# A transformer block on one core: every engine in source order from the expert queries on, with dependent steps spaced by units

## The chip, the cores and the metric

The kernel runs on one core of one Trainium2 chip. A core has TensorE (PE, matmuls), VectorE (DVE), ScalarE (ACT), GpSimd (POOL) and SyncE (SP, which here only issues DMAs), each with its own queue of instructions. The metric is the device time of one execution in microseconds; less is better.

## The reference

One layer on 256 tokens of width 2048, in float32: a mixer (sliding-window attention and an mLSTM, gated and merged), and then an expert retrieval (PEER) on the normed result. The change lies in the second part, which is this:

```python
xn = rms_norm(x)                                     # x: (256, 2048)
qp = (xn @ w_peer_q).reshape(T, 8, 2, 128)           # 8 heads, two halves
scores = einsum('thcd,hcnd->thcn', qp, peer_keys)    # 128 keys per half
s_top, i_top = top_k(scores, 16)
cand = s_top[:, :, 0, :, None] + s_top[:, :, 1, None, :]
top_s, pos = top_k(cand.reshape(T, 8, 256), 16)      # expert = i0 * 128 + i1
gates = softmax(top_s)
act = gelu(einsum('td,thkd->thk', xn, peer_u[idx]))  # exact gelu
out = x + einsum('thk,thkd->td', gates * act, peer_v[idx])
```

There are 16384 experts, so `peer_u` and `peer_v` have 16384 rows of 2048 numbers each.

## The kernel before

The retrieval is computed densely for 224 of the 256 tokens (ND). All of `u` is streamed once: 128 blocks of 128 experts ("expert i" below is such a block), each as two **units** of 128x1024 weights. A unit is loaded by SP into `raw` (4 buffers), split into two fp32r parts, `hi` by ScalarE (L89) and `lo` by VectorE (L90, from raw and hi), with 2 buffers each, and multiplied by TensorE: eight matmuls of hi with both parts of the tokens (L818) and eight of lo (L823). After an expert's second unit `sum_u` adds the two halves of the PSUM tile into `z` (ScalarE copy L214, VectorE add L215), and `act_u` takes the Gelu (L795, L797) into `W` (`wA` for the experts 0 to 79, `wB` for the others). The gates of each token are scattered into `W` four tokens at a time by `scatter`: VectorE compares a one-hot `A` (L1020), ScalarE makes a one-hot `B` times the gate with two activations per token (L1024, L1025), four matmuls multiply them (L1029), and VectorE (L1040) or ScalarE (L1042) puts the product into `W`. Where Gelu values already stand, it multiplies; where they don't yet, it copies and `act_u` multiplies later (L798). Then all of `v` is streamed in 256 units (L1090, L1092), with `W` split into a `ring` of fp32r entries (`split_w`).

The first 32 tokens (SP = 32) are computed by gathering: POOL fetches their experts' rows (`fetch`, L919) into six `slab` buffers, VectorE makes a dot product for each u row (`dot`, L949) and adds each weighted v row (`add_row`, L975). There are 128 such rows in each direction.

Ahead of the u stage come the queries: 32 units of `w_pq` (L174, L178), `score` (L767, L768) and the ranking, all of it on VectorE: `top16`, `pick16`, `decode`, `gates`, `lookup`, `turn`.

Stages are lists of units. `run` loads and splits the next unit and then calls `step` for the one before it. `step` first issues the unit's matmuls, then what was put in the list `later` in the step before, then one row of `rows_todo` when `pace[1]` reaches 1 (it grows by `row_rate` per unit), and then entries of `side`, as many as `pace[0]` pays for: it grows by the stage's rate per unit, is capped at 4, and each entry has a cost. `E0` is the expert from which the gates are scattered: the first run ends there, `drain` empties both lists, the ranking's memory is given back, and the second run begins.

The order of instructions on an engine is set by a planner, which puts ready instructions first by its own estimate of times. Before the change only VectorE is taken from it, from the queries to the end:

```python
    dve_order = tc.manual_schedule(engines={mybir.EngineType.DVE})
    dve_order.__enter__()
```

Under it VectorE runs its instructions in the order in which the source issues them. The queues of ScalarE, TensorE, POOL and SP are ordered by the planner (the gathers alone are kept in order by `keep`).

Of the kernel before, what the change touches and what calls it, by code (L numbers as in the profile page):

```python
# [8 lines left out]
F32 = mybir.dt.float32  # L9
# [3 lines left out]
AF = mybir.ActivationFunctionType  # L13
# [27 lines left out]
def hybrid_block_kernel(ctx: ExitStack, tc: tile.TileContext, a, out):  # L41
# [82 lines left out]
    def drain():  # L124
        flush()
        while side:
            tick()
# [18 lines left out]
    def run(units, rate=1.0):  # L146

        ready = None  # L150
        for u in units:
            nxt = (parts_of(load(u[0])), u[1])
            if ready:
                step(*ready, rate)
            ready = nxt
        if ready:
            step(*ready, rate)
# [571 lines left out]
        V.memset(part[c * SP:(c + 1) * SP], float(c))  # L729
    pair = exc.tile([P, SP], F32, name="pair")  # L730
    V.tensor_reduce(pair, ident.rearrange("p (c t) -> p t c", c=PARTS), axis=AX.X, op=OP.add)
    NSL = 6
    slab = [exc.tile([P, HD], F32, name=f"slab{j}") for j in range(NSL)]
    NA = 80
    wA = exc.tile([P, NA, ND], F32, name="wA")
# [2 lines left out]
    def load_xg():  # L738
        nc.sync.dma_start(wA[:, 0:KT], xgd)

    def norm_xg(c):
        xs = wA[:, 4 * c:4 * c + 4]
        V.tensor_mul(xs, xs, rb[:, SP:].unsqueeze(1).to_broadcast([P, 4, ND]))

    side += [(0.1, load_xg)] + [(1.0, lambda c=c: norm_xg(c)) for c in range(KT // 4)]
    second = []

    tks = ExitStack()
# [8 lines left out]
    def top16(vals, ov, oi):  # L757
        V.max(out=ov[:, 0:8], in_=vals)
        V.max_index(oi[:, 0:8], ov[:, 0:8], vals)
        V.match_replace(vals, ov[:, 0:8], vals, LOW)  # L760
        V.max(out=ov[:, 8:16], in_=vals)
        V.max_index(oi[:, 8:16], ov[:, 8:16], vals)

    def score(n, q):
        p2 = psd.tile([P, QU], F32, name="sd")
        for t in range(NT):
            PE.matmul(p2[:, t * NK:(t + 1) * NK], q[:, t * P:(t + 1) * P], keysT[:, n], start=True, stop=True)  # L767
        S.activation(sc[:, :, n], p2[:, 0:NT * NK].rearrange("p (t k) -> p t k", k=NK), AF.Copy)  # L768
        for t in range(NT):
            (side, second)[t].append((1.7, lambda t=t: top16(sc[:, t, n], st_[:, t, n], it_[:, t, n])))  # L770

    def evac_q(n):
        def g(ps):
            q = eb.tile([P, T], F32, name="z")
            total(q, ps[:, :T], ps[:, T:])
            V.tensor_mul(q, q, rb)
            later.append(lambda: score(n, q))
        return lambda ps: later.append(lambda: g(ps))
# [3 lines left out]
    def wv(i):  # L782
        return W[0][:, i] if i < NA else W[1][:, i - NA]
# [1 line left out]
    done = {"tok": 0, "e": 0}  # L785

    def sum_u(i, ps):
        z = eb.tile([P, ND], F32, name="z")
        total(z, ps[:, :ND], ps[:, ND:2 * ND])
        later.append(lambda: act_u(i, z))  # L790

    def act_u(i, z):
        k = done["tok"]
        if k < ND:
            S.activation(wv(i)[:, k:], z[:, k:], AF.Gelu)  # L795
        if k > 0:
            S.activation(z[:, :k], z[:, :k], AF.Gelu)  # L797
            V.tensor_mul(wv(i)[:, :k], wv(i)[:, :k], z[:, :k])  # L798
        done["e"] = i + 1

    own = {}
# [24 lines left out]
            return f  # L826
        return [(a["u"][i][:, h * HU:(h + 1) * HU], consume(i, h)) for i in range(i0, i1) for h in range(KT // per)]

    E0 = 66


    a16 = tk.tile([P, TOPK], F32, name="a16")
# [55 lines left out]
        V.tensor_mul(gv, gv, gs[:, 1].unsqueeze(2).to_broadcast([P, PH, TOPK]))  # L888

    def turn(t):  # L890
        pi = psd.tile([P, QU], F32, name="sd")
        for c in range(3):
            PE.transpose(pi[:, c * P:(c + 1) * P], iv[:, c], ident)
        V.tensor_copy(i0T[:, t * P:(t + 1) * P], pi[:, 0:P])
        V.tensor_scalar(i1T[:, t * P:(t + 1) * P], pi[:, P:2 * P], -1.0, None, op0=OP.mult)
        V.tensor_copy(gT[:, t * P:(t + 1) * P], pi[:, 2 * P:3 * P])
        V.tensor_scalar(ngT[:, t * P:(t + 1) * P], pi[:, 2 * P:3 * P], -1.0, None, op0=OP.mult)

    keep = tc.keep_in_program_order
    tables = {"u": a["ur"], "v": a["v"].rearrange("e (c d) -> (e c) d", d=HD)}

    def turn_to_grid():
# [11 lines left out]

    def fetch(table, s):
        ix = own["ix"]
        keep(G.indirect_dma_start(out=slab[s % NSL], out_offset=None, in_=tables[table],  # L919
                                  in_offset=bass.IndirectOffsetOnAxis(ap=ix[:, s:s + 1], axis=0)))  # L920

    def quarter_rows(dst, src):

# [55 lines left out]
    def choose():  # L979
        own["oh"] = tk.tile([P, 2, HG, TOPK, TOPK], F32, name="oh", tag="keysT")  # L980
        for t in range(NT):
            if t:
                side.extend(second)
            side.extend([(1.9, lambda t=t, h=h: pick16(t, h)) for h in range(PH)])
            side.extend([(2.6, lambda t=t: decode(t)), (0.9, lambda t=t: gates(t))])
            side.extend([(1.2, lookup(t, c, g)) for c in range(2) for g in range(2)])
            side.append((1.3, lambda t=t: turn(t)))
            if t == 0:
                side.extend([(1.0, own_index)] + [(1.0, lambda: None)] * 3 + [(0.5, own_rows)])
        own_x()  # L990

    def first(f, u):

        def g(parts):
            f()
            u[1](parts)
        return (u[0], g)

    row_rate[0] = 0.5
    dve_order = tc.manual_schedule(engines={mybir.EngineType.DVE})  # L1000
    dve_order.__enter__()
    units = []
    for n in range(2 * PH):
        units += ws_units(a["w_pq"][n], X2, evac_q(n))
    ue = u_units(0, E0)
    ue[0] = first(turn_to_grid, ue[0])
    ue[2] = first(choose, ue[2])
    run(units + ue, 1.0)
    drain()
    tks.close()  # L1010

# [4 lines left out]
    def scatter(t0):  # L1016

        A = eb.tile([P, TG, NK], F32, name="A")
        B = eb.tile([P, TG, NK], F32, name="B")
        V.tensor_tensor(A, iot.unsqueeze(1).to_broadcast([P, TG, NK]),  # L1020
                        i0T[:, t0:t0 + TG].unsqueeze(2).to_broadcast([P, TG, NK]), op=OP.is_equal)
        for j in range(TG):
            t = t0 + j
            S.activation(B[:, j], iot, AF.Square, bias=i1T[:, t:t + 1])  # L1024
            S.activation(B[:, j], B[:, j], AF.Relu, bias=gT[:, t:t + 1], scale=ngT[:, t:t + 1])  # L1025
        yield
        ps = psd.tile([P, TG, NK], F32, name="sd")
        for j in range(TG):
            PE.matmul(ps[:, j], B[:, j], A[:, j], start=True, stop=True)  # L1029
        yield  # L1030
        m = done["e"]
        c0 = t0 - SP
        for s, (lo, hi) in enumerate(((0, NA), (NA, NE))):
            for x0, x1, mul in ((lo, min(max(m, lo), hi), True), (max(min(m, hi), lo), hi, False)):
                if x1 <= x0:
                    continue
                dst = W[s][:, x0 - lo:x1 - lo, c0:c0 + TG]
                src = ps[:, :, x0:x1].rearrange("p t i -> p i t")
                if mul:
                    V.tensor_mul(dst, src, dst)  # L1040
                else:
                    S.activation(dst, src, AF.Copy)  # L1042
        done["tok"] = c0 + TG

    side += [(0.7, scatter(t0)) for t0 in range(SP, T, TG)]
    left = 2 * (NE - E0) - 6
    row_rate[0] = len(rows_todo) / left
    run(u_units(E0, NE), (ROW * len(rows_todo) + 2.1 * len(side)) / left)
    drain()
    while rows_todo:  # L1050
        rows_todo.pop(0)()

# [26 lines left out]
    def v_consume(i, h):  # L1081
        def f(parts):
            if i == 0:
                acc[h] = [(psd, pmm)[j % 2].tile([P, QU], F32, name=("sd", "mm")[j % 2]) for j in range(NB2)]
            if i % EG == 1:
                split_w((i - 1 + EG) % NE)
            hi, lo = parts
            both = ring[:, i % NR].rearrange("p s t -> p (s t)")
            for j in range(NB2):
                PE.matmul(acc[h][j][:, :2 * ND], hi[:, j * P:(j + 1) * P], both, start=(i == 0), stop=False)  # L1090
            for j in range(NB2):
                PE.matmul(acc[h][j][:, :ND], lo[:, j * P:(j + 1) * P], ring[:, i % NR, 0],  # L1092
                          start=False, stop=(i == NE - 1))
            if i == NE - 1:
                for j in range(NB2):
                    total(outT[h][j], acc[h][j][:, :ND], acc[h][j][:, ND:2 * ND])
        return f
# [16 lines left out]
            nc.sync.dma_start(out[0:SP, c * HD:(c + 1) * HD], own["x"][c * SP:(c + 1) * SP])  # L1114

    units = [(a["v"][i * P:(i + 1) * P, h * HU:(h + 1) * HU], v_consume(i, h)) for h in range(2) for i in range(NE)]
    ow = own_weights()
    next(ow), next(ow), next(ow, None)
    split_w(0)
    rows_todo += [lambda s=s: add_row(s) for s in range(NS)]  # L1120
    row_rate[0] = NS / (len(units) - 12)
    pace[1] = 0.0
    units[NE + 40] = first(load_x1, units[NE + 40])
    units[-3] = first(own_out, units[-3])
    run(units)
    flush()
    assert not rows_todo
    for q in range(4):
        finish(q)
    dve_order.__exit__(None, None, None)  # L1130


# [61 lines left out]
```

## Time and profile before

| | |
|---|---|
| time, median of 3 runs | 2233.15 us (2232.91 to 2233.73) |
| time of the profiled execution | 2231.89 us, its span 2230.1 us |
| TensorE matmul, weight load busy | 2132.3 us (96%), 1938.7 us (87%) |
| VectorE, ScalarE, GpSimd busy | 1689.4 (76%), 1283.9 (58%), 389.7 us (17%) |
| mean granted TensorE clock | 0.988 of full speed |
| DMA | 487.22 MB, mean 218 GB/s |

The time lies 1.8 us over the span, which counts from the first to the last instruction. TensorE's busy time comes from modelled ends of pipelined matmuls; the granted clock tells how far it ran at full speed. Stages by their first matmul: queries at 679.9, u at 799.0, the first scatter matmul at 1165.1, v at 1571.1 us.

### The profile page before, as it was taken

What the parts mean: (1) busy time and instruction counts of PE and PEld (TensorE: products, weight loads), DVE (VectorE), ACT (ScalarE), POOL (GpSimd) and SP (SyncE); (2) the same over time, 40 slices, a digit from 0 to 9 for tenths busy, and PEclk for the clock granted to TensorE, in tenths of its full rate; (3) what the DMA queues carried; (4) which work ended last, traced back from release to release, by engine and by line L of the source; (5) the groups of instructions that cost most, each with busy time, mean ns of one, the idle gap of its engine ahead of it and who ended that gap; (6) DMA issues with size and microseconds to landing.
All of it is one profiled execution on the core that took longest, in us unless ns stands there. A gap on an engine that the chain in (4) does not pass through costs nothing. (4 is left out here: it accounts for less than half of the span.)

```text
span 2230.1 us, 35017 instructions
## 1 busy us (share of the span) xinstructions
PE 2132.3 (96%) x12836; PEld 1938.7 (87%) x12836; DVE 1689.4 (76%) x2905; ACT 1283.9 (58%) x2238; POOL 389.7 (17%) x324
## 2 busy tenths in 40 slices
PE   6999999999997988999998999999999999999998
PEld 5887778888886878899888988889899999999998
DVE  7987687878886778788886777777677777777776
ACT  5755566556543444555558887887445555555544
POOL 3000000000031002333332222220322222322210
PEclk9999999999998999999999999999999999999999
DMA  5565544555575545777675665665777877877774
GB/s 201 189 190 169 166 159 163 179 190 186 199 249 197 171 153 177 255 262 257 234 244 197 216 218 203 217 217 203 250 262 266 262 269 262 292 263 267 262 260 162
DMA packets 138892, 487.22 MB, mean 218 GB/s; under 512 B 17712, under 2 KB 19968, under 8 KB 138240
## 3 DMA queue, kind: packets, MB, share of 16 engines
q1 hardware_dynamic: 115520, 415.43, 54.8%
q0 software_dynamic: 20896, 67.73, 9.5%
q8 instruction: 100, 1.64, 0.3%
q10 hardware_dynamic: 2304, 1.84, 0.2%
q14 instruction: 72, 0.59, 0.1%
HBM read 478.88 MB, written 6.05 MB: 217 GB/s over the span
## 5 line engine op out<-in xcount | busy, mean ns | idle before, releaser
L90 DVE TENSOR_TENSOR lo<-raw,hi 128x1024 fp32r<-128x1024 f32 x762 | 943.3, 1239 | 422.1 <-ACT hi L89 410.8
L89 ACT ACTIVATE hi<-raw 128x1024 fp32r<-128x1024 f32 x762 | 802.6, 1057 | 642.2 <-PE mm L1090 316.5
L818 PE MATMUL mm<-X,hi 128*128 128x448 f32 x2048 | 473.2, 374 | 26.5 <-ACT hi L89 21.4
L818 PEld LDWEIGHTS mm<-X,hi 128*128 128x128 f32 x2048 | 370.8, 191 | 57.7 <-ACT hi L89 28.3
L1090 PE MATMUL sd<-X,hi 128*128 128x448 f32 x1024 | 377.2, 368 | 2.5 <-DVE X L90 1.5
L1090 PE MATMUL mm<-X,hi 128*128 128x448 f32 x1024 | 375.5, 367 | 0.0
L174 PE MATMUL mm<-X,hi 128*128 128x512 f32 x1040 | 272.5, 403 | 15.4 <-ACT hi L89 8.7
L823 PEld LDWEIGHTS mm<-X,lo 128*128 128x128 f32 x2048 | 268.0, 192 | 22.1 <-DVE lo L90 15.3
L823 PE MATMUL mm<-X,lo 128*128 128x224 f32 x2048 | 270.8, 275 | 9.1 <-DVE lo L90 9.1
L919 POOL DMA_INDIRECT slab<-ur,oix x128 | 162.6, 1270 | 452.9 <-DVE slab L949 431.6
L1092 PE MATMUL mm<-X,lo 128*128 128x224 f32 x1024 | 241.5, 274 | 0.0
L1092 PE MATMUL sd<-X,lo 128*128 128x224 f32 x1024 | 239.7, 272 | 0.0
L174 PEld LDWEIGHTS mm<-X,hi 128*128 128x128 f32 x1040 | 190.4, 192 | 53.6 <-ACT hi L89 9.1
L919 POOL DMA_INDIRECT slab<-v,oix x128 | 150.6, 1176 | 480.5 <-DVE ox L975 432.5
L1090 PEld LDWEIGHTS sd<-X,hi 128*128 128x128 f32 x1024 | 193.9, 189 | 13.8 <-issue 1.7
L1090 PEld LDWEIGHTS mm<-X,hi 128*128 128x128 f32 x1024 | 193.9, 189 | 13.2
L1092 PEld LDWEIGHTS sd<-X,lo 128*128 128x128 f32 x1024 | 195.6, 191 | 3.8
L1092 PEld LDWEIGHTS mm<-X,lo 128*128 128x128 f32 x1024 | 195.7, 191 | 2.8
L178 PEld LDWEIGHTS mm<-X,lo 128*128 128x128 f32 x1040 | 143.3, 192 | 24.5 <-DVE lo L90 14.1
L178 PE MATMUL mm<-X,lo 128*128 128x256 f32 x1040 | 147.1, 284 | 13.7 <-DVE lo L90 13.7
L795 ACT ACTIVATE wA<-z 128x224 f32<-128x224 f32 (+7 forms) x80 | 30.9, 387 | 166.5 <-DVE z L215 166.5
L1025 ACT ACTIVATE B<-B,gT,ngT 128x128 f32<-128x128 f32 x224 | 102.4, 485 | 0.7
(326 smaller groups left out, 2389.7 us busy)
## 6 DMA issues: line engine op xcount, KB each, us to landing
raw<-u SPq DMA_DIRECT2D x256, 512.0 KB
raw<-v SPq DMA_DIRECT2D x256, 512.0 KB
raw<-w_g SPq DMA_DIRECT2D x64, 512.0 KB
raw<-w_tok SPq DMA_DIRECT2D x56, 512.0 KB
raw<-w_qk SPq DMA_DIRECT2D x32, 512.0 KB
raw<-w_o SPq DMA_DIRECT2D x32, 512.0 KB
raw<-w_pq SPq DMA_DIRECT2D x32, 512.0 KB
raw<-w_pa SPq DMA_DIRECT2D x16, 512.0 KB
```

The source lines that it names most:

```text
L89: S.activation(hi, src, AF.Copy)
L90: V.tensor_sub(lo, src, hi.bitcast(F32))
L174: PE.matmul(ps, hi[:, w], X[:, k].rearrange("p s t -> p (s t)"), start=(k == 0), stop=False)
L178: PE.matmul(ps[:, :T], lo[:, w], X[:, k, 0], start=False, stop=(k == kts - 1))
L795: S.activation(wv(i)[:, k:], z[:, k:], AF.Gelu)
L818: PE.matmul(ps[:, :2 * ND], hi[:, w], Xn[:, k].rearrange("p s t -> p (s t)"), start=(k == 0), stop=False)
L823: PE.matmul(ps[:, :ND], lo[:, w], Xn[:, k, 0], start=False, stop=(k == KT - 1))
L919: keep(G.indirect_dma_start(out=slab[s % NSL], out_offset=None, in_=tables[table], in_offset=bass.IndirectOffsetOnAxis(ap=ix[:, s:s + 1], ...
L1025: S.activation(B[:, j], B[:, j], AF.Relu, bias=gT[:, t:t + 1], scale=ngT[:, t:t + 1])
L1090: PE.matmul(acc[h][j][:, :2 * ND], hi[:, j * P:(j + 1) * P], both, start=(i == 0), stop=False)
L1092: PE.matmul(acc[h][j][:, :ND], lo[:, j * P:(j + 1) * P], ring[:, i % NR, 0], start=False, stop=(i == NE - 1))
```

## The change

All engines keep the source's order from the queries on, in one `manual_schedule()` without a list of engines, and steps that depend on each other are issued in different units: the Gelu one unit later than before, its multiplication one later again, the copy of a score and its ranking each one later, the turn's transposes one later. The load of `xg` is issued at once, and the four `norm_xg` stand at the query units 20, 22, 24 and 26. `E0` goes from 66 to 46, with rates to match. `scatter` yields after every two tokens of `B`, and copies before it multiplies. The runs over u and v become one; the own tokens' weights are made in its last u units. There are five slabs in place of six and three `z` buffers in place of two. The diff, cut to its core:

```diff
-    NSL = 6
+    NSL = 5
...
-    side += [(0.1, load_xg)] + [(1.0, lambda c=c: norm_xg(c)) for c in range(KT // 4)]
+    load_xg()
...
-        S.activation(sc[:, :, n], p2[:, 0:NT * NK].rearrange("p (t k) -> p t k", k=NK), AF.Copy)
-        for t in range(NT):
-            (side, second)[t].append((1.7, lambda t=t: top16(sc[:, t, n], st_[:, t, n], it_[:, t, n])))
+
+        def take():
+            S.activation(sc[:, :, n], p2[:, 0:NT * NK].rearrange("p (t k) -> p t k", k=NK), AF.Copy)
+            later.append(rank)
+
+        def rank():
+            for t in range(NT):
+                (side, second)[t].append((1.7, lambda t=t: top16(sc[:, t, n], st_[:, t, n], it_[:, t, n])))
+        later.append(take)
...
-        z = eb.tile([P, ND], F32, name="z")
+        z = eb.tile([P, ND], F32, name="z", bufs=3)
         total(z, ps[:, :ND], ps[:, ND:2 * ND])
-        later.append(lambda: act_u(i, z))
+        later.append(lambda: later.append(lambda: act_u(i, z)))
...
-            V.tensor_mul(wv(i)[:, :k], wv(i)[:, :k], z[:, :k])
+            later.append(lambda: V.tensor_mul(wv(i)[:, :k], wv(i)[:, :k], z[:, :k]))
...
-    E0 = 66
+    E0 = 46
...
     def turn(t):
+        later.append(lambda: turn_pe(t))
+
+    def turn_pe(t):
...
-                side.extend([(1.0, own_index)] + [(1.0, lambda: None)] * 3 + [(0.5, own_rows)])
+                side.extend([(1.0, own_index)] + [(1.0, lambda: None)] * 4 + [(0.5, own_rows)])
...
-    row_rate[0] = 0.5
-    dve_order = tc.manual_schedule(engines={mybir.EngineType.DVE})
-    dve_order.__enter__()
+    row_rate[0] = 0.12
+    in_order = tc.manual_schedule()
+    in_order.__enter__()
...
-    ue[2] = first(choose, ue[2])
-    run(units + ue, 1.0)
+    ue[4] = first(choose, ue[4])
+    for c in range(KT // 4):
+        units[20 + 2 * c] = first(lambda c=c: norm_xg(c), units[20 + 2 * c])
+    run(units + ue, 1.1)
     drain()
...
             S.activation(B[:, j], B[:, j], AF.Relu, bias=gT[:, t:t + 1], scale=ngT[:, t:t + 1])
-        yield
+            if j % 2:
+                yield
...
-        for s, (lo, hi) in enumerate(((0, NA), (NA, NE))):
-            for x0, x1, mul in ((lo, min(max(m, lo), hi), True), (max(min(m, hi), lo), hi, False)):
+        for mul, s in ((False, 0), (False, 1), (True, 0), (True, 1)):
+            lo, hi = ((0, NA), (NA, NE))[s]
+            for x0, x1 in (((lo, min(max(m, lo), hi)),) if mul else ((max(min(m, hi), lo), hi),)):
...
-    side += [(0.7, scatter(t0)) for t0 in range(SP, T, TG)]
+    side += [(0.55, scatter(t0)) for t0 in range(SP, T, TG)]
     left = 2 * (NE - E0) - 6
     row_rate[0] = len(rows_todo) / left
-    run(u_units(E0, NE), (ROW * len(rows_todo) + 2.1 * len(side)) / left)
-    drain()
-    while rows_todo:
-        rows_todo.pop(0)()
+    row_rate[0] = len(rows_todo) / (left - 4)
+    rate2 = (ROW * len(rows_todo) + 2.2 * len(side)) / left
+    units2 = u_units(E0, NE)
...
+    def begin_v():
+        flush()
+        while side or later:
+            drain()
+        split_w(0)
+
+    def end_dots():
+        while rows_todo:
+            rows_todo.pop(0)()
+
+    def begin_rows():
+        rows_todo.extend([lambda s=s: add_row(s) for s in range(NS)])
+        row_rate[0] = NS / (len(units) - 24)
+        pace[1] = 0.0
+
     ow = own_weights()
-    next(ow), next(ow), next(ow, None)
-    split_w(0)
-    rows_todo += [lambda s=s: add_row(s) for s in range(NS)]
-    row_rate[0] = NS / (len(units) - 12)
-    pace[1] = 0.0
+    units2[-9] = first(end_dots, units2[-9])
+    for j, f in ((-7, lambda: next(ow)), (-5, lambda: next(ow)), (-3, lambda: next(ow, None))):
+        units2[j] = first(f, units2[j])
+    units[0] = first(begin_v, units[0])
+    units[1] = first(begin_rows, units[1])
...
-    run(units)
+    run(units2 + units, rate2)
```

## Rows read from the trace of the kernel before

**Rows 1.** Stretches: us, busy (count) of PE, PEld, DVE, ACT, POOL; clock, DMA, GB/s.

```profile
679.00:704.00 25.00, 10.66 (x58) 8.54 (x57) 11.68 (x23) 5.97 (x10) 5.79 (x12) 0.80 0.61 206
799.00:1164.50 365.50, 346.51 (x2138) 321.43 (x2138) 304.38 (x652) 185.32 (x289) 110.00 (x68) 0.99 0.67 229
1000.00:1050.00 50.00, 50.00 (x320) 47.69 (x319) 44.20 (x114) 25.32 (x40) 15.95 (x10) 1.00 0.77 260
1164.50:1566.00 401.50, 374.81 (x2415) 354.26 (x2416) 289.44 (x554) 320.73 (x804) 76.96 (x73) 0.97 0.63 211
1572.00:2190.00 618.00, 617.07 (x3916) 587.39 (x3915) 445.52 (x443) 312.68 (x314) 148.75 (x127) 1.00 0.79 266
```

**Rows 2.** Timeline of TensorE, late units and a scatter group: start, us, engine, line.

```profile
1174.52 1.06 PE L1029 MATMUL sd<-A,B 128*128 128x128 f32 x8
1175.34 1.87 PE L818 MATMUL mm<-X,hi 128*128 128x448 f32 x8
...
1561.12 1.79 PE L818 MATMUL mm<-X,hi 128*128 128x448 f32 x8
1563.63 1.79 PE L818 MATMUL mm<-X,hi 128*128 128x448 f32 x8
```

**Rows 3.** Waits of 799 to 1164.5: total us, times, longest.

```profile
ACT wA L795 <- DVE z L215: 154.9, 64, 5.3
DVE lo L90 <- ACT hi L89: 42.3, 40, 3.3
```

**Rows 4.** Timeline of the u stage near 815.

```profile
812.90 0.33 ACT L214 ACTIVATE z<-mm 128x224 f32<-128x224 f32 x1
816.47 0.38 DVE L215 TENSOR_TENSOR z<-mm,z 128x224 f32<-128x224 f32 x1
816.89 0.39 ACT L795 ACTIVATE wA<-z 128x224 f32<-128x224 f32 x1 [3.65 <-DVE z L215]
817.19 2.00 ACT L89 ACTIVATE hi<-raw 128x1024 fp32r<-128x1024 f32 x2
818.28 1.89 PE L818 MATMUL mm<-X,hi 128*128 128x448 f32 x8 [0.52 <-ACT hi L89]
```

**Rows 5.** Waits of 1164.5 to 1566.

```profile
PE sd L1029 <- DVE A L1020: 15.0, 7, 3.9
```

**Rows 6.** Timeline of ScalarE in the scatter.

```profile
1180.33 0.69 ACT L1024 ACTIVATE B<-ones,i1T 128x128 f32<-128x128 f32 x2
...
1183.42 0.33 ACT L1042 ACTIVATE wB<-sd 128x192 f32<-128x192 f32 x1
1183.63 1.06 ACT L89 ACTIVATE hi<-raw 128x1024 fp32r<-128x1024 f32 x1
```

**Rows 7.** Timeline after the output projection, at norm_xg.

```profile
689.69 0.33 SPq L739 DMA_DIRECT2D wA<-xgd  x1
...
698.95 3.10 DVE L743 TENSOR_TENSOR wA<-wA,rb 128x896 f32<-128x896 f32 x3 [9.85 <-DMA wA<-xgd]
701.96 1.22 DVE L90 TENSOR_TENSOR lo<-raw,hi 128x1024 fp32r<-128x1024 f32 x1
...
703.23 2.08 PE L178 MATMUL mm<-X,lo 128*128 128x256 f32 x8 [13.65 <-DVE lo L90]
...
705.11 3.09 PE L174 MATMUL mm<-X,hi 128*128 128x512 f32 x8
...
709.35 2.09 PE L174 MATMUL mm<-X,hi 128*128 128x512 f32 x8
```

**Rows 8.** Timeline at the turn from u to v.

```profile
1566.71 0.94 ACT L89 ACTIVATE X<-wA 128x896 fp32r<-128x896 f32 x1
...
1569.84 1.15 DVE L90 TENSOR_TENSOR X<-wA,X 128x896 fp32r<-128x896 f32 x1
...
1571.13 0.71 PE L1090 MATMUL sd<-X,hi 128*128 128x448 f32 x1 [1.54 <-DVE X L90]
```

**Rows 9.** Group of the dots, 799 to 1164.5: busy, mean ns, idle before, releaser.

```profile
L949 DVE SCALAR_TENSOR_TENSOR slab<-slab,ox 128x512 f32<-128x512 f32 x49 | 33.6, 685 | 1.7 <-DMA slab<-ur,oix 1.7
```

More of the change, by code (lines that the diff above doesn't have):

```diff
@@ L767, in score @@
             PE.matmul(p2[:, t * NK:(t + 1) * NK], q[:, t * P:(t + 1) * P], keysT[:, n], start=True, stop=True)
-        S.activation(sc[:, :, n], p2[:, 0:NT * NK].rearrange("p (t k) -> p t k", k=NK), AF.Copy)
-        for t in range(NT):
-            (side, second)[t].append((1.7, lambda t=t: top16(sc[:, t, n], st_[:, t, n], it_[:, t, n])))
+        def take():
[5 more added lines that the diff above has]
+        later.append(take)
     def evac_q(n):
         def g(ps):
-            q = eb.tile([P, T], F32, name="z")
+            q = eb.tile([P, T], F32, name="z", bufs=3)
             total(q, ps[:, :T], ps[:, T:])
@@ L895, in turn @@
         V.tensor_scalar(i1T[:, t * P:(t + 1) * P], pi[:, P:2 * P], -1.0, None, op0=OP.mult)
+        V.tensor_scalar(ngT[:, t * P:(t + 1) * P], pi[:, 2 * P:3 * P], -1.0, None, op0=OP.mult)
         V.tensor_copy(gT[:, t * P:(t + 1) * P], pi[:, 2 * P:3 * P])
-        V.tensor_scalar(ngT[:, t * P:(t + 1) * P], pi[:, 2 * P:3 * P], -1.0, None, op0=OP.mult)
-    keep = tc.keep_in_program_order
     tables = {"u": a["ur"], "v": a["v"].rearrange("e (c d) -> (e c) d", d=HD)}
@@ L918, in fetch @@
         ix = own["ix"]
-        keep(G.indirect_dma_start(out=slab[s % NSL], out_offset=None, in_=tables[table],
-                                  in_offset=bass.IndirectOffsetOnAxis(ap=ix[:, s:s + 1], axis=0)))
+        G.indirect_dma_start(out=slab[s % NSL], out_offset=None, in_=tables[table],
+                             in_offset=bass.IndirectOffsetOnAxis(ap=ix[:, s:s + 1], axis=0))
     def quarter_rows(dst, src):
@@ L1129, in hybrid_block_kernel @@
         finish(q)
-    dve_order.__exit__(None, None, None)
+    in_order.__exit__(None, None, None)
 def kernel(**inputs):
```

## The prediction

> **What bounds the kernel now.** I read the page first, then a table of stretches, the waits of two of them, and the timeline at the places these name. TensorE is busy nearly throughout, but a busy share hides slow running, so count units: one 128x1024 slice of weights is 16 matmuls. In 1000 to 1050 the u stage begins 320 matmuls in 50 us, that is 20 units of 2.5 us [rows 1]. Two consecutive units late in the u stage start 2.51 us apart [rows 2]; I use 2.51 us as the price of a unit when nothing holds TensorE. A group of the scatter costs 0.82 us between its first matmul and the next unit's [rows 2]; I take 0.85 for the 56 groups, 47.6 us in all.
>
> With these two prices each stretch has a floor. The u stage before the scatter (units of experts 0 to 65, E0 = 66) runs from 799.0 to 1164.5: 132 x 2.51 = 331.3 us of work in 365.5 us, 34.2 lost (0.26 per unit). From there to 1566.0 are 124 units and 56 groups: 311.2 + 47.6 = 358.8 us in 401.5, 42.7 lost (0.76 per group). Together 76.9 us are lost in 767.0, and the reader sees in the table that no other engine is full there: VectorE is busy 304.4 of 365.5 and 289.4 of 401.5 us, ScalarE 185.3 and 320.7 [rows 1]. So the bound is waiting, not capacity.
>
> The waits say for whom. ScalarE stands 154.9 us in the first stretch before the Gelu of line 795, until VectorE has added z, and VectorE stands 42.3 us until ScalarE has made hi [rows 3]. The timeline shows the circle: ScalarE copies z at 812.90, then sits 3.65 us at the Gelu until VectorE, behind a pick16, has added z at 816.47; the Gelu runs at 816.89, and only then come two hi in a row, so TensorE's next hi matmul starts at 818.28 after an idle 0.52 us [rows 4]. In source order step() emits the next unit's hi ahead of the Gelu, so the planner had moved the Gelu forward: this is what a fixed order can take away. In the second stretch the scatter adds two waits: TensorE for the one-hot A, 15.0 us in 7 waits [rows 5], and ScalarE's eight activations of one group, in one piece with a copy, from 1180.33 to the hi at 1183.63 [rows 6].
>
> Two single places remain. At 689.69 the load of xg is issued, at 698.95 VectorE gets it and runs norm_xg ahead of the lo that TensorE needs, and TensorE stands 13.65 us [rows 7]. At the turn from u to v the last u unit starts at 1563.63 and so ends at 1566.14, and the first v matmul starts at 1571.13 [rows 2, 8]: 5.0 us, since the own tokens' weights stand on VectorE ahead of the split of the first ring entry.
>
> **The change part by part.** *norm_xg moved to query units 20 to 26.* The wait of 13.65 us goes, and with it the slow running behind it: the eight hi matmuls at 705.11 took 3.09 us against 2.09 at 709.35 [rows 7], 1.0 us more, behind an idle stretch with a granted clock of 0.80 in 679 to 704 [rows 1], so for part of it at the lower of its two levels, 1.2 GHz. Its four multiplications, three in 3.10 us, now lie two units apart beside query matmuls. What is late next: the weights behind the xg load on SP's queue. That transfer took 9.3 us, and three loaded units cover about 3 x 2.51 = 7.5; below lies 0, above 9.3. I take 3, just over what the cover leaves. Sum: -13.65 - 1.0 + 3 = -11.7.
>
> *Order on all engines, Gelu one unit later, its multiplication one later, score's copy and ranking one later.* This adds no instruction; a third z buffer pays for the longer life, with one slab less (6 to 5). With five slabs a gather is still four dots ahead, some 4 x 3.5 us at 0.79 dots per unit of 2.8 us; with six the dots waited 1.7 us in all [rows 9], so I cost it at nothing. Were a gather longer than that cover, each dot would hold VectorE. The wait of ScalarE for z ends: z was added a unit before.
>
> *E0 = 46.* Forty units and twenty experts move from the first stretch to the second. Stepping through the pace by hand, the ranking's costs (119 in all) at 1.1 per unit end at unit 122 of 124, with no remainder for the drain, and dots begin slowly (0.12 per unit), so 6 instead of 49 [rows 9] run before the scatter. VectorE's first stretch then holds 304.4 - 40 x 1.22 (lo) - 20 x 0.38 (z) - 43 x 0.685 (dots) = 218.5 us against a floor of 92 x 2.51 = 230.9: 95%. The second has a floor of 164 x 2.51 + 47.6 = 459.2; VectorE has 289.4 + 85.9, and at most 20 x 0.38 for twenty more experts in two pieces, 383 or 83%; ScalarE 320.7 + 40 x 1.06 + 20 x (0.33 + 0.39) = 378, 82% [rows 1, 4, 6, 7, 9].
>
> *One-hots two tokens at a time.* The piece of eight activations becomes two of four, so a hi waits behind half of it. The count stays. A and the matmul lie one tick further apart.
>
> *What the stages lose after it.* No row shows this order, so bounds. Below: 0, as in 1000 to 1050, where TensorE ran full with VectorE at 44.20 of 50 [rows 1]. Above: the same losses as now, 92 x 0.26 + 56 x 0.76 = 66.5 us. VectorE at 95% in one stretch is above the row that lost nothing, the second stretch is below it; bursts remain (decode and gates in one step, the table load at gates). I take 0.1 per unit, nearer to zero: 25.6 us. The stop between the two runs at E0 stays, and in source order it is a chain after TensorE's last matmul: copy 0.33, add 0.38, Gelu 0.39, hi 1.06, with gaps 2.5 us [rows 4, 6]. So the u stage takes 690.1 + 2.5 + 25.6 = 718.2 instead of 767.0: -48.8.
>
> *u and v in one run.* Own weights come seven units earlier, and at the turn only the ring's split is left, 0.94 on ScalarE and 1.15 on VectorE, with gaps 2.3 us instead of 5.0 [rows 8]: -2.7. It can't start earlier, as the ring takes the slot of Xn. The v stage itself already runs full and its order hardly matters; I cost the slightly faster rows there (0.55 for 0.52 per unit) at nothing, since VectorE is busy only 445.52 of 618 us in it [rows 1].
>
> Sum against the profiled execution (2231.89 us; span 2230.1): -11.7 - 48.8 - 2.7 = -63.2, so 2168.7. It stands 1.3 us below the median of the runs, so 2170 us.
>
> **The rivals.** *The order leaves the waits* (the same losses per unit and group, by another instruction each time). Against it: the wait of 154.9 us has one cause, which the spacing removes [rows 3, 4]. For it: VectorE at 95%. Then the u stage takes 690.1 + 2.5 + 66.5, and the time is 2211.
>
> *Less room than the units say, or a full VectorE.* Weight loads fill 47.69 of 50 us at the full rate, and 321.43 + 354.26 us in the two stretches [rows 1]; at that share the work is 708 us, not 690, so only 59 of 767 are lost, and the sum ends 18 us later, at 2188. Against it: a load that ran slowly counts as work there. (The Trainium skill, Perfetto Trace Analysis, Identifying the Most-Contended Engine, takes the weight loads' share and not the matmuls' as the measure of headroom; by it this is the sum.) A full VectorE leads to the same region: if its waits for hi stay in proportion, 42.3 x 92 / 132 = 29.5, its first stretch needs 248.0 for a floor of 230.9, 17.1 lost instead of 9.2: 2178.
>
> *A head-of-line wait makes it slower.* The scatter's copies now stand on ScalarE where the source has them, ahead of the next hi, and wait for scatter matmuls that stand behind 16 matmuls of a unit. In the worst alignment a hi starts not when its slot comes free but after 2.51 + 0.85 + 0.33 (the copy), behind a piece of four activations (half of 3.1 us [rows 6]) and with its own 1.06: ready at 6.3 us, where TensorE asks for it at 2 x 2.51 + 0.85 = 5.9. That is 0.4 us per group, 22 us, and only brings 2192. It turns the change slower from 63.2 / 56 = 1.1 us per group beyond what I have charged; at 1.5 us the time is 2170 + 84 = 2254. ScalarE's 18% of free time speaks against that. The Trainium skill (TensorE: Matmul & The Clock Gate, Architectural detail) says that ScalarE and VectorE are strict first-in first-out; the 3.65 us before a Gelu with two hi behind it agree [rows 4], and no row shows it for the copies.
>
> *The change doesn't do what it says*: were ScalarE already in source order, only the spacing would act. The Gelu ahead of both hi says that it isn't.
>
> **How the numbers follow.** Forecast (2147 to 2178) 0.52; less room or a full VectorE (2178 to 2195) 0.22; the waits stay (2195 to 2224) 0.13; head of line, not faster 0.08; better than 2147 0.05. With loss 0 the sum gives 2144, with all of it 2211, and the xg load moves it by -3 to +6. The range 2147 to 2210 leaves out the better cases and some 0.14 above it. A difference under 0.2% (4.5 us) is about what a measurement of this kernel can't tell from no change. Faster takes all but the head-of-line case and a small part of the stayed waits: 0.89; same 0.04; slower 0.07.
>
> **What would show it.** Right: no wait of lo behind norm_xg near 690; the wait of the wA Gelu for z nearly gone and hi at its slot's release; the first stretch near 242 us for 92 units, the second near 477 us; the turn to v about 2 to 3 us; the granted clock at 1.00 in the u stage. Wrong: TensorE's waits for hi or lo of the same sum as now, a drain of ranking left over at expert 46, ScalarE standing before the scatter's copies, or new waits for raw.

## The result, and the profile after

The changed kernel takes 2179.82 us (median of 4 runs, 2176.99 to 2179.99) where the kernel before took 2233.03 (2230.89 to 2233.73): a ratio of 0.976, 95% interval 0.9743 to 0.9777, 53 us less. The profiled execution took 2179.96 us with a span of 2178.2 us, 51.9 less than the span before.

By stages, between the same marks as in the table of before: the first u matmul starts at 780.7 us (18.3 earlier), the first v matmul at 1507.8, so the u stage with its turn takes 727.1 us in place of 772.1 (45.0 less), and from there to the end 670.4 us in place of 659.0, 11.4 **more**. The forecast had -11.7, -51.5 and 0.

The stretches of the kernel after, with the columns of [rows 1]:

```profile
679.00:704.00 25.00, 23.51 (x138) 20.37 (x137) 16.80 (x37) 11.54 (x18) 6.25 (x12) 1.00 0.91 309
780.70:1023.00 242.30, 237.35 (x1482) 222.37 (x1482) 221.24 (x510) 127.71 (x191) 43.48 (x24) 0.99 0.61 209
1025.00:1505.00 480.00, 470.35 (x3074) 446.65 (x3075) 371.10 (x715) 402.52 (x933) 142.17 (x122) 1.00 0.73 245
1507.80:2167.00 659.20, 650.30 (x4096) 618.58 (x4097) 461.76 (x461) 326.79 (x333) 143.60 (x123) 0.99 0.76 254
```

The reader sees TensorE with 138 matmuls where it had 58 in the 25 us at norm_xg, its clock there at full speed instead of 0.80, and the v stage with more idle time than before (650.30 of 659.20 us, to the last v matmul; 617.07 of 618.00 in the part of v in [rows 1]).

The waits of 780.5 to 1024 us (total us, times, longest), which answer [rows 3]:

```profile
ACT hi L89 <- PE mm L824: 93.7, 77, 2.7
DVE lo L90 <- ACT hi L89: 9.2, 14, 1.4
PE mm L829 <- DVE lo L90: 4.0, 7, 1.5
ACT wA L801 <- DVE z L215: 0.2, 1, 0.2
```

and those of 1024 to 1506 us, which answer [rows 5]:

```profile
DVE lo L90 <- ACT hi L89: 104.3, 88, 4.4
ACT wB L1054 <- PE sd L1040: 11.6, 10, 3.2
PE mm L824 <- ACT hi L89: 8.0, 9, 2.3
PE sd L1040 <- ACT B L1035: 2.1, 5, 0.7
```

ScalarE's 154.9 us before the Gelu are 0.2 here, and 0.2 again in the second stretch. What its hi waits for now is a slot that TensorE's matmuls free (93.7 us), which is a sign that the forecast named for being right. TensorE's 15.0 us for A are gone. TensorE's 8.0 us for hi hold the stop at expert 46 (2.30 of them).

The timeline at norm_xg, for [rows 7]:

```profile
689.92 0.33 SPq L739 DMA_DIRECT2D wA<-xgd  x1
...
701.41 1.06 ACT L89 ACTIVATE hi<-raw 128x1024 fp32r<-128x1024 f32 x1 [4.29 <-DMA raw<-w_pq]
701.90 1.11 PE L178 MATMUL mm<-X,lo 128*128 128x256 f32 x8
```

The xg load stands at the same place and the next weights are late behind it: ScalarE waits 4.29 us for raw. TensorE has no wait there, since it still has split units to multiply.

The turn from u to v, for [rows 8]:

```profile
1502.61 1.79 PE L824 MATMUL mm<-X,hi 128*128 128x448 f32 x8
...
1505.40 0.93 ACT L89 ACTIVATE X<-wA 128x896 fp32r<-128x896 f32 x1
...
1506.67 1.08 DVE L90 TENSOR_TENSOR X<-wA,X 128x896 fp32r<-128x896 f32 x1
...
1507.81 0.47 PE L1101 MATMUL sd<-X,hi 128*128 128x448 f32 x1 [2.53 <-DVE X L90]
```

With 2.51 us for the last unit the turn takes 1507.81 - 1502.61 - 2.51 = 2.7 us, where it took 5.0.

**Where the v stage lost.** Two stops of TensorE, both for a weight load that came late from SP's queue. First the timeline of SP, and one line each of ScalarE and TensorE behind it:

```profile
1906.79 17.92 SPq L94 DMA_DIRECT2D raw<-v  x8
1924.76 0.47 SPq L1080 DMA_DIRECT2D wA<-x1d  x1
1925.27 0.49 SPq L1081 DMA_DIRECT2D wA<-x1d  x1
1925.81 2.55 SPq L1083 DMA_DIRECT2D wA<-x1d  x4
1928.46 15.59 SPq L94 DMA_DIRECT2D raw<-v  x5
...
1941.38 1.06 ACT L89 ACTIVATE hi<-raw 128x1024 fp32r<-128x1024 f32 x1 [8.24 <-DMA raw<-v]
...
1942.49 0.53 PE L1101 MATMUL sd<-X,hi 128*128 128x448 f32 x1 [4.53 <-ACT hi L89]
```

The three parts of the residual (`load_x1`) are issued in one piece, 768, 1024 and 256 KB, and the 512 KB blocks of v queue behind them. In the kernel before the planner had put the same three issues at 1911.56, 1931.67 and 1941.72, with weight loads between them. The second stop is at the end. A wait of SP in 2100 to 2178 us:

```profile
SPq L1125 <- DVE ox L1123: 10.2, 1, 10.2
```

and the timeline of VectorE, SP, ScalarE and TensorE there:

```profile
2154.31 0.68 DVE L1123 TENSOR_TENSOR ox<-ox,wA 128x512 f32<-128x512 f32 x1
2155.03 1.74 SPq L1125 DMA_DIRECT2D out<-ox  x4
...
2156.87 0.39 SPq L94 DMA_DIRECT2D raw<-v  x1
...
2161.11 1.06 ACT L89 ACTIVATE hi<-raw 128x1024 fp32r<-128x1024 f32 x1 [7.12 <-DMA raw<-v]
...
2162.22 0.74 PE L1101 MATMUL sd<-X,hi 128*128 128x448 f32 x1 [4.26 <-ACT hi L89]
2162.75 0.57 PE L1101 MATMUL mm<-X,hi 128*128 128x448 f32 x1
```

SP stands 10.2 us before the four stores of `own_out`, because they wait for VectorE's sum at 2154.31, and the last load of v stands behind them in the queue. Before the change the stores were issued at 2212.76, behind every load; SP waited 7.7 us for the same sum there, with no load left to hold.

### The profile page after: what moved, and what is told of

Its sections match the earlier page's. It is cut to its first block, busy times and chain, and to the rows that moved or that the text cites. A ratio compares the mean times of both kernels' runs of the same rounds, so it can differ in the third digit from the quotient of the medians.

```text
span 2178.2 us, 34889 instructions
## 1 busy us (share of the span) xinstructions
PE 2120.5 (97%) x12836; PEld 1934.2 (89%) x12836; DVE 1685.0 (77%) x2915; ACT 1307.7 (60%) x2269; POOL 382.4 (18%) x324
## 5 line engine op out<-in xcount | busy, mean ns | idle before, releaser
L90 DVE TENSOR_TENSOR lo<-raw,hi 128x1024 fp32r<-128x1024 f32 x762 | 936.6, 1230 | 423.2 <-ACT hi L89 416.3
L824 PE MATMUL mm<-X,hi 128*128 128x448 f32 x2048 | 467.5, 371 | 11.4 <-ACT hi L89 8.9
L1101 PE MATMUL sd<-X,hi 128*128 128x448 f32 x1024 | 378.6, 370 | 11.4 <-ACT hi L89 8.8
L927 POOL DMA_INDIRECT slab<-ur,oix x128 | 150.8, 1178 | 402.9 <-DVE slab L957 367.5
L1035 ACT ACTIVATE B<-B,gT,ngT 128x128 f32<-128x128 f32 x224 | 110.8, 494 | 7.5
```

The costliest lines, as they stand in the source:

```text
L90: V.tensor_sub(lo, src, hi.bitcast(F32))
L824: PE.matmul(ps[:, :2 * ND], hi[:, w], Xn[:, k].rearrange("p s t -> p (s t)"), start=(k == 0), stop=False)
```

## The experiments

Twelve kernels, each measured beside the kernel before, which took 2230.5 to 2232.0 us there and 2233.0 beside the changed kernel; so a difference of 2.5 us or less to the changed kernel is not read as one. "u" is from the first u matmul to the first v matmul, "v" from there to the end of the span, both of the profiled execution. u less the floor of the forecast (256 units of 2.51 and 56 groups of 0.85, 690.1 us) is "lost".

| kernel | us | ratio (95%) | u | lost | v |
|---|---|---|---|---|---|
| before | 2233.0 | 1 | 772.1 | 82.0 | 659.0 |
| changed | 2179.8 | 0.976 (0.9743 to 0.9777) | 727.1 | 37.0 | 670.4 |
| out_late | 2172.6 | 0.9739 (0.9722 to 0.9755) | 727.2 | 37.1 | 664.0 |
| x1_spread | 2173.7 | 0.9746 (0.9729 to 0.9762) | 726.6 | 36.5 | 664.7 |
| both | 2167.9 | 0.9718 (0.9702 to 0.9735) | 726.7 | 36.6 | 658.9 |
| sp_free | 2166.8 | 0.971 (0.9694 to 0.9727) | 727.0 | 36.9 | 658.0 |
| only_dve | 2191.3 | 0.9818 (0.9801 to 0.9834) | 752.3 | 62.2 | 657.3 |
| no_gap | 2181.1 | 0.9783 (0.9766 to 0.9799) | 726.9 | 36.8 | 670.5 |
| e0_66 | 2187.0 | 0.9804 (0.9788 to 0.9821) | 734.4 | 44.3 | 671.0 |
| one_piece | 2216.3 | 0.9936 (0.9919 to 0.9952) | 763.0 | 72.9 | 671.1 |
| b_norm | 2216.9 | 0.9936 (0.9919 to 0.9952) | 770.9 | 80.8 | 658.8 |
| b_norm_gap | 2212.1 | 0.9913 (0.9896 to 0.9929) | 766.5 | 76.4 | 659.0 |
| b_order | 2319.3 | 1.0386 (1.0369 to 1.0404) | 849.0 | 158.9 | 671.7 |
| b_norm_order_gap | 2302.5 | 1.0325 (1.0308 to 1.0343) | 848.4 | 158.3 | 669.2 |

Two groups stand out in the last column. With SP's queue ordered by the planner v takes 657 to 659 us, and with SP in source order and both calls where the change has them 669 to 672.

### SP's order and the v stage

Three kernels change only when the changed kernel issues the two transfers. `out_late` moves the stores behind the last load, `x1_spread` splits the residual's load over three units, `both` does the two. The second cut leaves out the edit by which `load_x1` returns its three parts:

```diff
-    units[-3] = first(own_out, units[-3])
+    units[-1] = first(own_out, units[-1])
```

```diff
-    units[NE + 40] = first(load_x1, units[NE + 40])
+    for j, f in enumerate(load_x1()):
+        units[NE + 40 + 8 * j] = first(f, units[NE + 40 + 8 * j])
```

> The changed kernel with one edit: the four output DMAs of the own tokens and their addition stand at the last v unit instead of the third last, behind the last load of weights on SP's queue. Theory (SP's source order puts DMAs that wait ahead of a load): the idle 4.26 us before the last unit's first hi matmul and its slow running (4.8 us for a unit of 2.5) go, 6.6 us, so 2173 us, and only TensorE's stop near 1940 is left in the v stage. Rival (the v stage lost its time to VectorE's order or to five slabs): the last load lands as late as before, 2180 us.

> The changed kernel with one edit: the three parts of load_x1 (0.75, 1 and 0.25 MB) stand at the v units 168, 176 and 184 instead of all at 168. Theory (in source order they stand in one piece ahead of the next loads of weights, where the planner had put 20 and 8 us between them): the stop of 4.53 us at 1938 and the slow running behind it go, 6 to 7 us, 2173 us. Rival (the bytes cost their time wherever they stand, the DMA share being 0.98 there): the stop is split into smaller ones of the same sum, 2178 to 2180 us.

> Both edits together. Theory: the v stage is back at its length before the change (some 659 us from its first matmul to the end of the span, where the changed kernel has 670.4), so 2179.8 - 12 to 13 = 2167 us. Rival: 2178 to 2180 us, or only one of the two gains.

The v stage falls by 6.4, 5.7 and 11.5 us, so each stop is worth about 6 and the two add up to the whole loss. The fourth kernel leaves the source's calls alone and gives SP's queue back to the planner:

```diff
-    in_order = tc.manual_schedule()
+    in_order = tc.manual_schedule(engines={mybir.EngineType.DVE, mybir.EngineType.Activation, mybir.EngineType.PE, mybir.EngineType.Pool})
```

> The changed kernel with the source's order on TensorE, ScalarE, VectorE and GpSimd, while SP's queue is the planner's again. Theory (the loss in the v stage is SP's order alone): both stops of the v stage go without moving either DMA in the source, 2167 to 2172 us. Rival (another engine's order makes them): 2178 to 2181 us. If the planner's order of loads is worse elsewhere, waits for raw show it in the u stage.

It takes 2166.8 us, with v at 658.0 and u unchanged. In it SP issues the residual's first part at 1847.1 us, the second at 1867.2 and the rest from 1877.2 on. The line of the first (issue time in ns, first and last start):

```profile
L1080 SPq DMA_DIRECT2D wA<-x1d x1: 326/326/326, 1847.1 to 1847.1; - x1
```

and the timeline of SP near the end:

```profile
2135.11 5.35 SPq L94 DMA_DIRECT2D raw<-v  x3
2148.28 1.74 SPq L1125 DMA_DIRECT2D out<-ox  x4
```

The last loads stand ahead of the stores. So the loss in v is the order of SP's queue alone, and the changed kernel is beaten by some 12 to 13 us if SP is left out of the change or the two calls are moved: `both` and `sp_free` are the fastest kernels here. All four came out within 1 us of the theory.

### The order without the rest, and the rest without the order

`b_order` is the kernel before with source order on all engines; the `keep` on the gathers goes with it, as in the change, and nothing else differs. `b_norm` is the kernel before with the load of xg and the four norm_xg placed as in the change, and the old order. `b_norm_gap` adds the Gelu one unit later (with three z buffers and five slabs), still in the old order. `b_norm_order_gap` is that kernel with source order on all engines. The edit of the order:

```diff
-    dve_order = tc.manual_schedule(engines={mybir.EngineType.DVE})
+    dve_order = tc.manual_schedule()
```

> The kernel before with one edit: the source's order on all engines instead of on VectorE alone (no step moved, E0 = 66, six slabs). Theory (the planner had moved the Gelu ahead of two hi, and any source order puts one hi ahead of it): ScalarE's wait of 154.9 us for z falls to under 60, the u stage from 799.0 to 1566 (767 us) to some 735 to 745, while the stop at norm_xg stays, and the two stops of the v stage appear only if load_x1 and own_out stand in the way there too: 2200 to 2215 us. Rival (the spacing by units makes the gain, not the order): 2228 to 2236 us.

> The kernel before with one edit: load_xg at once and the four norm_xg at the query units 20 to 26, VectorE alone in source order. Theory: the stop of 13.65 us and the slow running behind it go and nothing else changes, so 2233.0 - 14 to 18 = 2215 to 2219 us. Rival (the loads behind xg are late in place of it): 2222 to 2228 us.

> As the run before, and the Gelu one unit later (with the third z buffer and five slabs); ScalarE is still ordered by the planner. Theory (the order is what counts, the planner moves the Gelu forward whatever the source says): 2213 to 2219 us, with ScalarE's wait for z over 100 us as before. Rival (the spacing alone removes the wait): the wait under 40 us and 2185 to 2195 us.

> The kernel before with three parts of the change: norm_xg moved, source order on all engines, and the Gelu one unit later (three z buffers, five slabs). Scatter, score and E0 stay as before. Theory: the order alone lost 77 us in the u stage mostly at the scatter's ScalarE copies, which stand ahead of the next hi and wait for VectorE's multiplications (76.7 and 25.1 us), and only 32.7 us of ScalarE's waits were the Gelu's for z; so the gap rescues only that part: 2319 - 15 (norm_xg) - 20 to 33 = 2270 to 2285 us, still slower than before, with the waits of line 1042 as long as with the order alone. Rival: the Gelu's spacing is what makes the order pay: at or below the 2212 us that the same spacing took with ScalarE's queue by the planner.

`b_order` was a miss on both sides: 3.9% slower than before, where neither theory had it above 2236. What the theory said of the Gelu did come: ScalarE's wait for z falls from 154.9 us to

```profile
ACT wA L795 <- DVE z L215: 31.1, 20, 3.7
```

from 797 to 1152 us. The first stretch is 11 us shorter than that of before (354.9 to 366.0 us up to the first scatter matmul), but the second takes 494.1 instead of 406.1 us. The waits of ScalarE from 1152 to 1645 us say where:

```profile
ACT wB L1042 <- DVE wB L1040: 76.7, 37, 3.3
ACT wA L1042 <- DVE wA L1040: 25.1, 12, 2.4
```

and the timeline of VectorE (L1040, L90), ScalarE and TensorE shows one of them:

```profile
1208.87 0.45 DVE L1040 TENSOR_TENSOR wA<-sd,wA 128x288 f32<-128x288 f32 x1
...
1209.36 0.20 ACT L1042 ACTIVATE wA<-sd 128x32 f32<-128x32 f32 x1 [2.33 <-DVE wA L1040]
1209.45 0.33 ACT L1042 ACTIVATE wB<-sd 128x192 f32<-128x192 f32 x1
1209.66 1.06 ACT L89 ACTIVATE hi<-raw 128x1024 fp32r<-128x1024 f32 x1
...
1210.75 1.23 DVE L90 TENSOR_TENSOR lo<-raw,hi 128x1024 fp32r<-128x1024 f32 x1 [1.43 <-ACT hi L89]
...
1212.83 2.38 PE L1029 MATMUL sd<-A,B 128*128 128x128 f32 x8 [3.21 <-ACT B L1025]
```

In the source of before the multiplication of a group (VectorE) comes ahead of its copy (ScalarE), so the copy stands 2.33 us for it, the hi behind the copy waits too, and VectorE's next lo waits for that hi: two queues in order hold each other, and after them TensorE stands 3.21 us. This is the place that the forecast's head-of-line rival named, a copy ahead of the next hi; but that rival had the copy wait for the scatter's matmuls, and here it waits for VectorE. The Trainium skill (TensorE: Matmul & The Clock Gate, Architectural detail) says that ScalarE and VectorE are strict first-in first-out; the 2.33 us, with a hi queued directly behind, agree for the copies, which no row of before showed.

`b_norm` takes 14.8 us off the start of the u stage (784.2 for 799.0) and 1.2 off u, as its theory had it. `b_norm_gap` is another 4.8 us faster, 1 us better than its theory, but ScalarE's waits before the Gelu stay at 164.7 and 33.9 us: the planner moves the Gelu forward wherever the source has it. `b_norm_order_gap` shows that the Gelu's spacing does not rescue the order either: u takes 848.4 us, as with the order alone, and the copies wait 87.1 and 26.2 us. It came out slower than the 2270 to 2285 that I had expected.

`only_dve` is the changed kernel with source order on VectorE alone, as before, except that the gathers, which `keep` held in order there, are left to the planner too:

```diff
-    in_order = tc.manual_schedule()
+    in_order = tc.manual_schedule(engines={mybir.EngineType.DVE})
```

> The changed kernel with the source's order on VectorE alone, all other engines ordered by the planner, all else as changed. Theory (order): the waits for z and for hi come back, the u stage takes over 750 us, 2195 to 2215 us; the v stage has no stop. Rival (spacing and E0 alone): 2165 to 2180 us.

With every other edit in place but the old order u takes 752.3 us, and ScalarE's waits from 779 to 1532 us are back:

```profile
ACT wA L801 <- DVE z L215: 159.3, 68, 5.3
ACT wB L801 <- DVE z L215: 56.4, 36, 2.8
```

The mechanism is that of the theory, but the time is 4 us under the range that it gave; the rival's 2165 to 2180 is missed as well. The new source without the order thus takes 19.8 of the 45.0 us off u. The order of ScalarE, TensorE and POOL is worth the other 25 (752.3 to 727.1), and 24.5 us of time against `sp_free`; on the old source the order costs 87 us. Which of the three engines it is was not tried apart; the waits that go are ScalarE's.

### Single parts undone

`no_gap` puts the Gelu back into the unit after its sum, `e0_66` the scatter back to expert 66 (with the first run's paces of before), `one_piece` the one-hots of a group back into one piece:

```diff
-        later.append(lambda: later.append(lambda: act_u(i, z)))
+        later.append(lambda: act_u(i, z))
```

```diff
-    E0 = 46
+    E0 = 66
-    row_rate[0] = 0.12
+    row_rate[0] = 0.5
-    run(units + ue, 1.1)
+    run(units + ue, 1.0)
```

```diff
-            if j % 2:
-                yield
+        yield
-    side += [(0.55, scatter(t0)) for t0 in range(SP, T, TG)]
+    side += [(0.7, scatter(t0)) for t0 in range(SP, T, TG)]
-    rate2 = (ROW * len(rows_todo) + 2.2 * len(side)) / left
+    rate2 = (ROW * len(rows_todo) + 2.1 * len(side)) / left
```

> The changed kernel (2179.8 us) with the Gelu in the unit after its sum again, and not one unit later. Theory: in source order the Gelu then stands on ScalarE ahead of a hi and waits for VectorE's sum, which stands behind a piece of ranking: some 25 us of waits over 92 units of the first stretch, as the 32.7 us over 132 with the order alone, part of it hidden by the second hi buffer: 2188 to 2205 us. Rival: with the ranking and the scatter spaced, the hi still comes in time: 2177 to 2183 us.

> The changed kernel (2179.8 us) with the scatter from expert 66 again and the paces of the first run as before (1.0 for the ranking, 0.5 for the dots). Theory: the 56 groups then lie in 124 units, ScalarE has 320.7 us of work in a floor of 358.8 (89%) against 82% now, and a copy that waits holds a hi more often; the first stretch has more room for the lookups: together 5 to 15 us slower, 2185 to 2195 us. Rival: the place of the scatter costs nothing once the order is fixed: 2175 to 2184 us; or the room for the lookups is worth more, and it is faster than 2175 us.

> The changed kernel (2179.8 us) with the eight activations of a group's one-hots in one piece again (and the cost and rate of a group as before). Theory: a piece takes 3.1 us on ScalarE where a unit lasts 2.51, so a hi behind a copy and a whole piece comes 1 to 2 us late in a part of the 56 groups: 10 to 40 us slower, 2190 to 2220 us. Rival: two hi buffers cover one piece: 2176 to 2184 us.

`no_gap` can't be told from the changed kernel (2178.97 to 2184.41 against 2176.99 to 2179.99): the theory's 2188 to 2205 is missed, and the rival holds. ScalarE's wait before the wA Gelu grows from 0.2 to 26.8 us, and u stays at 726.9: in source order the Gelu stands behind the next hi, and the wait is taken from ScalarE's free time. `e0_66` costs 7.2 us, inside the range expected: its second stretch loses 0.53 us per group (29.5 over its floor of 358.8) where the changed kernel loses 0.37. `one_piece` costs 36.5 us and takes two thirds of the change's gain. Its timeline of ScalarE and TensorE, the sixteen activations of two pieces cut to the first and the last:

```profile
1237.75 1.06 ACT L89 ACTIVATE hi<-raw 128x1024 fp32r<-128x1024 f32 x1 [0.56 <-PE mm L824]
1238.72 0.39 ACT L1034 ACTIVATE B<-ones,i1T 128x128 f32<-128x128 f32 x1
...
1244.88 0.49 ACT L1035 ACTIVATE B<-B,gT,ngT 128x128 f32<-128x128 f32 x1
1245.28 1.04 ACT L89 ACTIVATE hi<-raw 128x1024 fp32r<-128x1024 f32 x1
...
1246.37 1.89 PE L824 MATMUL mm<-X,hi 128*128 128x448 f32 x8 [1.85 <-ACT hi L89]
```

Two pieces of 3.28 us stand on ScalarE without a hi between them, 6.56 us against two units of 5.0. TensorE's waits for hi from 1029 to 1543 us are 28.3 us in 20, and the granted clock of that stretch is 0.97 where the changed kernel has 1.00 in 1030 to 1507.

## Why the forecast was right, and which step failed

The forecast was 2170, and the time 9.8 us over it. It was right in the main: the floor of units and groups held, and what u loses above it fell from 82.0 to 37.0 us. But 2179.8 lies above its first case (2147 to 2178), in the band given to "less room or a full VectorE", and neither of these was the cause: VectorE's waits for hi in the first stretch are 9.2 us, not the 29.5 of that rival. Two of its signs of being wrong did show: ScalarE stands before the scatter's copies (11.6 + 3.9 us), and the v stage has new waits for raw. By its own steps, in the profiled execution:

- **norm_xg: -11.7 forecast, -18.3 measured.** The wait and the slow running are as forecast; the 3 us charged for the weights behind the xg load were mis-sized. They are late (4.29 us on ScalarE), but TensorE doesn't wait. Without that term the sum is -14.7, and `b_norm`, which makes this move alone, measures -14.8. Of the other 3.5 us, 2.9 are TensorE's wait at the first u matmul for VectorE's split of the tokens: 5.0 us in the kernel before and in `b_norm`, 2.1 in the changed kernel and in `only_dve`. In the kernel before VectorE waits 1.61 us for the copy of a score and ranks it ahead of that split; with copy and ranking a unit later each, it has no such wait there.
- **The u stage: 718.2 forecast, 1505.1 - 780.7 = 724.4 measured.** The first stretch with the stop at expert 46 takes 244.6 us (242.6 forecast), the second 479.8 (475.6). TensorE's listed waits in the second, without the stop, are 8.7 us of the 20.6 lost, and the 11 units that hold them lose 12.2. The unit at 1031.39, behind the stop, loses 1.6 (clocks of 0.80 and 0.87 in 1029 to 1033 and 1033 to 1040 us). The 48 other groups without a wait lose 2.2: the median unit with a group takes 3.41 us, so a group costs 0.90 and not 0.85. The last 4.6 us are spread over the 108 units with neither. The weight-load rival, 2188, is not what happened: u takes 11.8 us less than the 690.1 + 18 + 2.5 + 25.6 us that it needs.
- **Why u gets shorter.** The forecast gave the end of ScalarE's wait to the spacing. It is the order that ends it (`b_order`, `only_dve`, `no_gap`); the extra unit for the Gelu adds nothing that can be measured in the changed kernel. And the step charged the order as free of new stalls. That holds only with the rest of the change: on the old source the order is 3.9% slower. Of the 121.3 us between `b_norm_order_gap` and the changed kernel in u, the split one-hots account for 36 when undone and E0 for 7. Most of what is left belongs, I believe, to copying ahead of multiplying: the copies' waits for VectorE (87.1 + 26.2 us) have become 11.6 + 3.9 us for the scatter's matmul. `one_piece`, which copies first but has the one-hots in one piece, shows no wait of a copy for VectorE either, and its u is 85.4 us shorter than that of `b_norm_order_gap`. But copying first was not tried alone, nor the later score or the later multiplication, so the share of each stays open.
- **The turn: 2.3 forecast, 2.7 measured.**
- **The v stage: 0 forecast, +11.4 measured.** This is the step that failed: "already runs full and its order hardly matters". The argument looked at VectorE's free time and not at SP, whose queue is part of the order and feeds the bound engine. The head-of-line wait that the rival placed on ScalarE came on SP. `out_late`, `x1_spread` and `sp_free` show it. With it gone, `both` takes 2167.9 us. That this lies only 2 us from 2170 is luck in part, since the misses of the first two steps cancel.

The sum of these misses, -6.6 + 6.2 + 0.4 + 11.4, is the 11.3 us by which the span missed, but for rounding.

## What to carry to other kernels

Source order on all engines is only as good as the source: ahead of fixing it, look for each piece on an in-order queue that is longer than the slack of the instruction behind it (eight activations ahead of a hi), and for each pair of engines that wait for each other within a group (copy behind multiplication). Count the queue that issues the loads among the engines: a store that waits, or a large transfer in one piece, holds every load behind it. Read a long wait as a cost only if the bound engine waits behind it: 26.8 us on ScalarE cost nothing, one late load cost 6 us.

## What the runs showed of the hardware

**A stop costs more than its length.** After the stops of 4.53 and 4.26 us the matmuls of line 1101 take 0.57 us where they took 0.36, at a granted clock of

```profile
1942.40:1946.10 3.70, 3.61 (x12) 3.28 (x13) 3.63 (x4) 2.26 (x4) 0.47 (x1) 0.55 0.68 257
2162.20:2166.20 4.00, 3.98 (x13) 3.64 (x13) 1.24 (x2) 0.41 (x2) 0.00 (x0) 0.50 0.00 0
```

(stretches, columns as above), the lower of the two levels, 1.2 GHz, nearly throughout. The unit that begins at 1942.49 takes until 1946.67, 4.18 us for 2.51, so that stop cost some 6.2 us; the v stage without it is 5.7 us shorter.

**VectorE and GpSimd block each other whole.** The first stretch lost 11.4 us up to its last matmul (1023.0 - 780.7 - 230.9), 6.8 of it in the 16 units from 838.99 to 865.39 and from 999.67 to 1020.23 us, where the lookups run. The timeline of VectorE and POOL in two of them:

```profile
841.91 3.32 POOL L884 TENSOR_TENSOR oh<-oh,itf 128x1024 f32<-128x1024 f32 x1 [2.30 <-DVE oh L881]
...
844.32 2.00 DVE L90 TENSOR_TENSOR lo<-raw,hi 128x1024 fp32r<-128x1024 f32 x1
...
849.93 1.21 DVE L90 TENSOR_TENSOR lo<-raw,hi 128x1024 fp32r<-128x1024 f32 x1
...
850.09 3.32 POOL L884 TENSOR_TENSOR oh<-oh,itf 128x1024 f32<-128x1024 f32 x1 [4.86 <-DVE oh L881]
...
851.07 3.42 DVE L881 TENSOR_TENSOR oh<-abf,a 128x1024 f32<-128x1024 f32 x1
854.41 1.21 DVE L90 TENSOR_TENSOR lo<-raw,hi 128x1024 fp32r<-128x1024 f32 x1
```

The lo that began ahead of POOL's multiplication takes 1.21 us; the comparison that begins inside it takes 3.42 us, 2.2 more than it takes otherwise, and ends 1.08 us after POOL does, about its own length. The lo at 844.32 does the same in 2.00 us. So it is with all eight multiplications: the instruction of VectorE with two inputs in SBUF that begins inside one (five times a lo, which TensorE waits for) ends 1.08 us after it. The multiplication seems to wait in its turn: each of the eight begins 0.04 to 0.22 us into a lo, takes 3.27 to 3.45 us, and ends 2.26 to 2.28 us after that lo. A reduction (L886, one input) at 843.19 ran inside a multiplication in 1.21 us. The Trainium skill (SBUF — State Buffer, Who interferes with whom) says that an instruction of VectorE with two inputs in SBUF contends with a GpSimd instruction that reads SBUF, and that the one that comes second waits for the whole of the other; these rows agree. Not all of the 6.8 us need be this: three transposes stand in each of the two stretches. No kernel here moves that multiplication to another engine, so what the eight lookups would give back is left open.
